# Hymba hybrid layer on one core: key and score slots padded from 4,224 to 4,352 bytes

## The chip, the cores and the metric

The kernel runs on one core of one Trainium2 chip. The metric is the device time of one execution in microseconds; lower is better. The time before is 1485.66 us, the median of 3 runs (1484.82 to 1486.38).

## The reference, cut to what matters

One decoder layer on 256 tokens of width 2,048, in float32. An input projection feeds two head groups side by side (a state-space part and a sparse attention), their outputs go through one output projection, and a convolutional feed-forward part with 5,632 channels follows.

```python
h = rms_norm(x, mix_norm_w)
proj = h @ w_in                                   # 2048 -> 10320 columns
z, xbc, dt_raw, q, kc, vc, ksl, vsl, kwn, vwn, gl = split(proj)
y_ssm  = rms_norm(ssd(silu(conv(xbc)), dt) * silu(z), ssm_norm_w)
y_attn = rms_norm(nsa_attention(q, kc, vc, ksl, vsl, kwn, vwn, gl), attn_norm_w)
x = x + concat([y_attn, y_ssm]) @ w_out           # 4096 -> 2048
u = conv(rms_norm(x, ffn_norm_w) @ w_up)          # 2048 -> 11264
gate, val = split(u, 2)
x = x + (silu(gate) * val) @ w_down               # 5632 -> 2048
return rms_norm(x, final_norm_w)
```

## The kernel before, in words

**The matmuls.** Every weight is read once from memory, in pieces of 512 KB (tile `raw`, 128 partitions x 1,024 floats). ScalarE rounds a piece to TensorE's reduced float32 (`whi`, fp32r), and VectorE forms what the rounding left (`wlo`). The activations are kept in the same two parts. A product is then three: high by high, high by low, low by high. A matmul here has a *stationary* operand, 128 columns that are loaded into the array (an LDWEIGHTS of its own), and a *moving* operand that streams past it, 512 or 256 columns. The 128 columns for the next matmul are loaded while the present one streams.

There are two layouts, and they swap the roles:

- **Channel pairs** (`chan_pair`, L332): the weights are stationary and the activations move. A step works on one piece. L343 issues 8 matmuls of 512 columns (4 slices of k by 2 blocks of channels; the moving tile is `hcat` or, in the feed-forward part, `hcatf`, high and low part side by side), and L346 issues 8 of 256 columns with `wlo` stationary. The 36 channel pairs of the input projection and the 44 of `w_up` have 4 steps each: 320 steps, 2,560 matmuls of 512 columns and 2,560 of 256. 56 of either kind, in the first steps, are recorded under L87, which is a helper's line.
- **Token groups**: the activations are stationary, 128 tokens at a time, and the weights move, always 512 columns. These are `tok_group` (L368, matmuls in L380 and L384) for the two value projections (stationary tile `hcat`) and for `w_out` (stationary `ya`, the attention's half, and `ys`, the state-space half), `prod_steps` (L1110, matmuls in L1122 and L1125) for `w_down` (stationary `act`), and `seven_steps` (L1159, matmuls in L1170 to L1172), which saves products in `w_down` by sums of activations (stationary `act` or `sums`). Together 1,965 matmuls of 512 columns. A step of `tok_group` or `prod_steps` has 8 matmuls with `whi` and then 4 with `wlo`.

**The order of the work.** One list of steps sets it. Step i's matmuls are issued in program order; its load is issued 7 steps ahead, its rounding 3 steps ahead (`LOADS`, `AHEAD`, L29). Side work (attention, state-space heads, convolutions) is cut into pieces that are issued between steps. The order of `w_down` is the string in L1353: p is a pair of steps of `prod_steps` on one `act` tile (act6, act7, act8, then act9 and so on), s is `seven_steps` on act0, act1 and so on, 21 matmuls each.

**The places in SBUF.** Most tiles live in the pool `gp` (L55) under fixed slots: `big(n, ...)` is slot Gn and `wide(n, ...)` is slot Hn. A slot is as large as its largest tile, and slots lie one behind the other in the order of their first use; the pools `stage` (tiles `raw`, `whi`, `wlo`) and `tmp` follow. All partitions have the same layout. Most slots have 4,096 or 8,192 bytes, whole multiples of 256. Two kinds of tile are 4,224 bytes, 16.5 times 256: `kcat` (keys, L633, slots G20 to G23) and `p1` (scores, L741, slots G27 and G28). Behind each of these six slots the addresses move by half of 256.

The addresses in the built program, from the start of a partition, with their remainder modulo 256:

| slots, in the order of their places | tiles that a large matmul reads there | before | after |
|---|---|---|---|
| G33, G16 | act21; xdt0, v00, ya0, act4 | 224 | 224 |
| G20 (4,224 bytes before) | kcat0, ya8, act8 | 224 | 224 |
| H0 to H3 | hcat, hcatf, sums2, sums3 | 96 | 224 |
| G12 to G15 | bc, blk | 96 | 224 |
| G17 to G19, G24 to G26 | v, ya2 to ya6, qp, ys0 to ys4, act5 to act7, act12 to act14 | 96 | 224 |
| G27 (4,224 before) | ys6, act15 | 96 | 224 |
| G28 (4,224 before) | ys8, act16 | 224 | 224 |
| G29, G30, G31, G8, G32, G9, G10, G11 | ys10 to ys14, pt, act0 to act3, act17 to act20 | 96 | 224 |
| G21 (4,224 before) | kcat1, ya10, act9 | 96 | 224 |
| G22 (4,224 before) | kcat2, ya12, act10 | 224 | 224 |
| G23 (4,224 before) | kcat3, ya14, act11 | 96 | 224 |
| pool stage | raw, whi, wlo | 224 | 224 |
| pool tmp | rt, u, acc, gate, bc1 (hold some of the sums) | 224 | 224 |

Inside these tiles the operands of the large matmuls start at multiples of 512 bytes, so an operand has its tile's remainder. In the table's terms, a large matmul's two operands lie **half a turn apart** (224 and 96) or at the **same remainder** (224 and 224).

Before, all 5,120 matmuls of the channel pairs are half a turn apart (`whi` or `wlo` at 224, `hcat` at 96). Of the 1,965 of the token groups 1,518 are half a turn apart, and 447 are at the same remainder: those with ya0, ya8, ya12, ys8, act4, act8, act10, act16, act21 and the sums in the pool tmp as the stationary tile.

Of the kernel before, what the change touches and what calls it, by code (L numbers as in the profile page):

```python
# [10 lines left out]
F32 = mybir.dt.float32  # L11
F32R = mybir.dt.float32r
# [4 lines left out]
P = 128  # L17
# [25 lines left out]
def hymba_kernel(  # L43
# [18 lines left out]
    def big(slot, shape, dtype, name):  # L62
        return gp.tile(shape, dtype, tag=f"G{slot}", name=name)
# [28 lines left out]
    def split(hi, lo, src):  # L92
        A.activation(hi, src, AF.Copy)
        V.tensor_tensor(lo, src, hi.bitcast(F32), op=ALU.subtract)
# [378 lines left out]
    def join_x(ps, scale=None, out_=None):  # L473

        u = join(ps, scale, out_)
        V.tensor_tensor(u, u, r1bc[0], op=ALU.mult)
        return u
# [115 lines left out]
    kcat = [None] * NG  # L593
# [35 lines left out]
    def kx_evac(b, g0):  # L629
        def evac(c, ps):  # L630
            g = g0 + c
            if kcat[g] is None:
                kt = big(20 + g, [P, 2, 528], F32R, f"kcat{g}")  # L633
                V.memset(kt[:, :, 15:16].bitcast(F32), 0.0)
                kcat[g] = kt
            u = join_x(ps).rearrange("p (s k) -> p s k", s=2)
            dv_ = [kcat[g][:, hl, 16:528].rearrange("p (s b k) -> p s b k", s=2, b=2)[:, :, b] for hl in range(2)]
            split(dv_[0], dv_[1], u)
        return evac
# [98 lines left out]
    def attention(g):  # L738
        q = [qp[2 * g], qp[2 * g + 1]]
        p0 = big(29, [P, 4, 272], F32, "p0")  # L740
        p1 = [big(27 + i, [P, 2, 528], F32, f"p1{i}") for i in range(2)]  # L741
        nm = [tmp.tile([P, 4, 3], F32, tag=f"nm{t}", name=f"nm{t}", bufs=1) for t in range(NT)]
        sm = [tmp.tile([P, 4, 3], F32, tag=f"sm{t}", name=f"sm{t}", bufs=1) for t in range(NT)]
        slope = [2.0 ** (-0.5 * (4 * g + h + 1)) for h in range(4)]
# [155 lines left out]
    def q_evac(pr):  # L900
        def evac(c, ps):
            if c == 0:
                if pr >= 3:
                    while (pr - 3) // 2 not in scored:
                        tick(1)
                qp[pr] = big(24 + pr % 3, [P, 2, 2, L], F32R, "qp")
            u = join_x(ps, scale=SCALE)
            split(qp[pr][:, c, 0], qp[pr][:, c, 1], u)
            if pr % 2 == 1 and c == 1:
                aux.append(attention(pr // 2))  # L910
        return evac
# [607 lines left out]
```

## Time and profile before

| | |
|---|---|
| median of 3 runs | 1485.66 us |
| the profiled execution, from its first to its last instruction | 1483.0 us |
| what lies around that span, against the median | 2.7 us |
| TensorE busy, matmuls | 1470.2 us of the span (99%) |
| VectorE busy | 1152.9 us (78%) |
| ScalarE busy | 889.0 us (60%) |
| DMA engines, share | about 60%, 188 GB/s |

How to read it: the duration that the profile gives for a matmul is from its start to its modelled end, some 390 ns for 512 columns, and neighbours overlap, so it is not what a matmul costs. What one costs in a dense stream is the distance from its start to the start of the next. The timeline merges equal matmuls into one row (start, length, count), so that the distance between the starts of two rows, divided by the matmuls in between, is the cost of one. Buffer numbers are left out in the profile: `act` is any of act0 to act21, and which one it is follows from the order of the steps.

### The profile page before, as it was taken

What the parts mean: (1) busy time and instruction counts of PE and PEld (TensorE: products, weight loads), DVE (VectorE), ACT (ScalarE), POOL (GpSimd) and SP (SyncE); (2) the same over time, 40 slices, a digit from 0 to 9 for tenths busy, and PEclk for the clock granted to TensorE, in tenths of its full rate; (3) what the DMA queues carried; (4) which work ended last, traced back from release to release, by engine and by line L of the source; (5) the groups of instructions that cost most, each with busy time, mean ns of one, the idle gap of its engine ahead of it and who ended that gap; (6) DMA issues with size and microseconds to landing.
All of it is one profiled execution on the core that took longest, in us unless ns stands there. A gap on an engine that the chain in (4) does not pass through costs nothing.

```text
span 1483.0 us, 21817 instructions
## 1 busy us (share of the span) xinstructions
PE 1470.2 (99%) x7936; PEld 1254.5 (85%) x7936; DVE 1152.9 (78%) x1894; ACT 889.0 (60%) x1446; POOL 3.6 (0%) x19
## 2 busy tenths in 40 slices
PE   9999999999999999999999999999999999999997
PEld 8888888888888888888888888888888888788886
DVE  7999799866898898555477777777777779978777
ACT  6768556655677697444365555555555556555544
POOL 0000000000000000000000000000000000000000
PEclk9999999999999999999999999999999999999999
DMA  8666667775454546555556666666656665565664
GB/s 256 170 189 209 199 192 237 228 230 157 143 143 135 168 138 216 186 186 188 190 173 191 190 184 186 187 186 195 186 185 186 189 194 185 192 210 188 204 199 142
DMA packets 222683, 278.47 MB, mean 188 GB/s; under 512 B 13176, under 2 KB 186864, under 8 KB 222448
## 3 DMA queue, kind: packets, MB, share of 16 engines
q1 hardware_dynamic: 220800, 272.59, 59.3%
q10 hardware_dynamic: 1776, 4.50, 0.9%
q8 instruction: 62, 1.02, 0.3%
q14 instruction: 45, 0.37, 0.1%
HBM read 274.92 MB, written 2.13 MB: 187 GB/s over the span
## 4 chain that ended last, share of the span: by engine, by line
PE 93%; DVE 3%; DMA 1%; ACT 1%; issue 1%; DVEq 0%; ACTq 0%; SPq 0%
PE mm L343 37%; PE mm L346 19%; PE mm L380 10%; PE mm L384 5%; PE aux L1122 4%; PE mm L1122 3%; PE aux L1125 2%; PE mm L1125 2%; DVE wlo L320 1%; DMA raw<-in_w_in_dram 1%; PE aux L1172 1%; PE aux L1171 1%; PE mm L1172 1%; PE aux L1170 1%; PE mm L1170 1%
## 5 line engine op out<-in xcount | busy, mean ns | idle before, releaser
L320 DVE TENSOR_TENSOR wlo<-raw,whi 128x1024 fp32r<-128x1024 f32 x408 | 496.9, 1221 | 244.6 <-ACT whi L314 243.1
L314 ACT ACTIVATE whi<-raw 128x1024 fp32r<-128x1024 f32 x408 | 430.7, 1057 | 412.9 <-PE mm L343 218.7
L343 PE MATMUL mm<-hcatf,whi 128*128 128x512 f32 x1408 | 356.8, 395 | 0.0
L343 PEld LDWEIGHTS mm<-hcatf,whi 128*128 128x128 f32 x1408 | 252.7, 188 | 46.5
L343 PE MATMUL mm<-hcat,whi 128*128 128x512 f32 x1096 | 282.4, 397 | 0.0
L343 PEld LDWEIGHTS mm<-hcat,whi 128*128 128x128 f32 x1096 | 197.7, 188 | 37.4 <-ACT rt L361 0.3
L346 PEld LDWEIGHTS mm<-hcatf,wlo 128*128 128x128 f32 x1408 | 191.7, 188 | 16.2
L346 PE MATMUL mm<-hcatf,wlo 128*128 128x256 f32 x1408 | 195.8, 282 | 0.0
L346 PEld LDWEIGHTS mm<-hcat,wlo 128*128 128x128 f32 x1096 | 149.6, 188 | 12.3
L346 PE MATMUL mm<-hcat,wlo 128*128 128x256 f32 x1096 | 153.8, 282 | 0.0
L1148 ACT ACTIVATE whi<-raw 128x1024 fp32r<-128x1024 f32 x88 | 91.6, 1057 | 67.4 <-DVE raw L1203 18.8
L1154 DVE TENSOR_TENSOR wlo<-raw,whi 128x1024 fp32r<-128x1024 f32 x88 | 105.4, 1221 | 12.6 <-ACT whi L1148 11.8
L380 PE MATMUL mm<-whi,ya 128*128 128x512 f32 x256 | 66.4, 398 | 0.0
L380 PE MATMUL mm<-whi,ys 128*128 128x512 f32 x256 | 64.5, 394 | 0.0
L1122 PE MATMUL aux<-whi,act 128*128 128x512 f32 x256 | 64.4, 394 | 0.0
L1122 PE MATMUL mm<-whi,act 128*128 128x512 f32 x232 | 59.5, 394 | 0.0
L380 PEld LDWEIGHTS mm<-whi,ys 128*128 128x128 f32 x256 | 48.2, 188 | 11.1
L1122 PEld LDWEIGHTS aux<-whi,act 128*128 128x128 f32 x256 | 48.1, 188 | 10.9
L380 PEld LDWEIGHTS mm<-whi,ya 128*128 128x128 f32 x256 | 47.3, 189 | 10.1
L1122 PEld LDWEIGHTS mm<-whi,act 128*128 128x128 f32 x232 | 43.7, 188 | 9.9
L362 DVE TENSOR_TENSOR u<-mm,rt 128x256 f32<-128x256 f32 x136 | 51.1, 417 | 0.2
L361 ACT ACTIVATE rt<-mm 128x256 f32<-128x256 f32 x144 | 46.6, 371 | 3.4 <-PE mm L346 2.2
(398 smaller groups left out, 1778.7 us busy)
## 6 DMA issues: line engine op xcount, KB each, us to landing
raw<-in_w_up_dram SPq DMA_DIRECT2D x176, 512.0 KB, 3.6
raw<-in_w_in_dram SPq DMA_DIRECT2D x160, 512.0 KB, 4.0
raw<-in_w_down_dram SPq DMA_DIRECT2D x88, 512.0 KB, 5.1
raw<-in_w_out_dram SPq DMA_DIRECT2D x64, 512.0 KB, 3.7
acq<-acum_d ACTq DMA_DIRECT2D x8, 512.0 KB, 5.8
raw<-in_cmp_w_k_dram SPq DMA_DIRECT2D x8, 512.0 KB, 4.6
raw<-in_cmp_w_v_dram SPq DMA_DIRECT2D x8, 512.0 KB, 4.6
x<-in_x_dram SPq DMA_DIRECT2D x4, 512.0 KB, 7.0
```

Source lines behind the costliest of these rows:

```text
L314: A.activation(hv, s.raw, AF.Copy)
L320: V.tensor_tensor(lv, s.raw, s.w[0].bitcast(F32), op=ALU.subtract)
L343: T.matmul(st["ps"][c], hv[:, kl, c * P:(c + 1) * P], k_of(k), start=(k == 0), stop=False)
L346: T.matmul(st["ps"][c][:, 256:512], lv[:, kl, c * P:(c + 1) * P], k_of(k)[:, 0, :], start=False, stop=(k == nk - 1))
L361: A.activation(rt, ps[:, 256:512], AF.Copy)
L362: V.tensor_tensor(u, ps[:, 0:256], rt, op=ALU.add)
L380: T.matmul(st["ps"][t], act(k)[:, hl, t * P:(t + 1) * P], hv[:, kl], start=(k == 0 and hl == 0), stop=False)
L384: T.matmul(st["ps"][t], act(k)[:, 0, t * P:(t + 1) * P], lv[:, kl], start=False, stop=(k == nk - 1))
L1122: T.matmul(x_[2 * t + n], act(k)[:, hl, t * P:(t + 1) * P], hv[:, n], start=(first and kl == 0 and hl == 0), stop=False)
L1125: T.matmul(x_[2 * t + n], act(k)[:, 0, t * P:(t + 1) * P], lv[:, n], start=False, stop=(last and kl == 1))
L1148: A.activation(hv[:, 0:n], src()[:, 0:n], AF.Copy)
L1154: V.tensor_tensor(lv[:, 0:n], src()[:, 0:n], s.w[0].bitcast(F32)[:, 0:n], op=ALU.subtract)
```

## The change

Two shapes grow from 528 to 544 floats in the last dimension. The 16 added floats are never read or written: all views end at column 528 as before. The six slots G20 to G23, G27 and G28 grow from 4,224 to 4,352 bytes (17 times 256), slot G29 keeps its 4,352, and everything behind the first of them moves up by 128 to 768 bytes. The instructions, their order on every engine, their shapes and their waits are the same in both programs; only addresses differ.

```diff
@@ -630,7 +630,7 @@
         def evac(c, ps):
             g = g0 + c
             if kcat[g] is None:
-                kt = big(20 + g, [P, 2, 528], F32R, f"kcat{g}")
+                kt = big(20 + g, [P, 2, 544], F32R, f"kcat{g}")
                 V.memset(kt[:, :, 15:16].bitcast(F32), 0.0)
                 kcat[g] = kt
@@ -738,7 +738,7 @@
     def attention(g):
         q = [qp[2 * g], qp[2 * g + 1]]
         p0 = big(29, [P, 4, 272], F32, "p0")
-        p1 = [big(27 + i, [P, 2, 528], F32, f"p1{i}") for i in range(2)]
+        p1 = [big(27 + i, [P, 2, 544], F32, f"p1{i}") for i in range(2)]
```

## The prediction

> **What bounds the kernel now.** First the profile's page: the span, the engines, the granted clock, the costliest groups.
>
> ```profile
> span 1483.0 us, 21817 instructions
> PE 1470.2 (99%) x7936; PEld 1254.5 (85%) x7936; DVE 1152.9 (78%) x1894; ACT 889.0 (60%) x1446; POOL 3.6 (0%) x19
> PEclk9999999999999999999999999999999999999999
> ...
> L343 PE MATMUL mm<-hcatf,whi 128*128 128x512 f32 x1408 | 356.8, 395 | 0.0
> ...
> L346 PE MATMUL mm<-hcatf,wlo 128*128 128x256 f32 x1408 | 195.8, 282 | 0.0
> ```
>
> TensorE is busy from end to end at the full clock (9 is 90% or more). The last number of a group is its idle time: 0.0 us in front of both. The chain that ended last runs 93% through TensorE, and of all groups of TensorE waits the longest comes to 1.4 us:
>
> ```profile
> PE 93%; DVE 3%; DMA 1%; ACT 1%; issue 1%; DVEq 0%; ACTq 0%; SPq 0%
> ```
>
> ```profile
> PE aux L497 <- DVE bc L94: 1.4, 1, 1.4
> ```
>
> So the time is the sum of what the matmuls cost, start to start. What one costs is in the timeline of TensorE (start in us, length, count). First a stretch of w_down, where the weights stream and the activations are stationary. By the order of L1353 it begins inside act7's pair of steps; then come act8's two steps, 21 matmuls on act0, act9's two steps and act10's first.
>
> ```profile
> 1247.27 2.02 PE L1122 MATMUL aux<-whi,act 128*128 128x512 f32 x8
> 1249.13 1.08 PE L1125 MATMUL aux<-wlo,act 128*128 128x512 f32 x4
> 1250.05 1.98 PE L1122 MATMUL aux<-whi,act 128*128 128x512 f32 x8
> 1251.86 1.07 PE L1125 MATMUL aux<-wlo,act 128*128 128x512 f32 x4
> 1252.77 1.98 PE L1122 MATMUL aux<-whi,act 128*128 128x512 f32 x8
> ...
> 1255.49 0.41 PE L1170 MATMUL mm<-whi,act 128*128 128x512 f32 x1
> ...
> 1260.37 2.03 PE L1122 MATMUL aux<-whi,act 128*128 128x512 f32 x8
> ...
> 1265.96 1.99 PE L1122 MATMUL aux<-whi,act 128*128 128x512 f32 x8
> 1267.79 1.07 PE L1125 MATMUL aux<-wlo,act 128*128 128x512 f32 x4
> 1268.69 1.52 PE L1122 MATMUL aux<-whi,act 128*128 128x512 f32 x6
> ```
>
> A step has 12 equal matmuls. act7's last step takes 1250.05 - 1247.27 = 2.78 us, or 231.7 ns for each. Both of act8's take 2.72 us (1252.77 - 1250.05, 1255.49 - 1252.77): 226.7 ns. act9's take 5.59 us for two (1265.96 - 1260.37), 2.795 each: 232.9 ns. act10's first takes 2.73 us. Same instructions, same engines at work beside them, clock the same. What differs is the table of addresses: act8 and act10 lie at 224 modulo 256, as the moving whi and wlo do, while act7 and act9 lie at 96. With both operands at one remainder a matmul of 512 columns costs 226.7 ns; half a turn apart it costs about 232.5. That is what the change can earn, since it brings every large pair to one remainder.
>
> The gain needs a run-in. In w_out, ys8 and ya8 are both at 224 as well; here are, by the order of the steps, a step of ys8 and then the first step of ya8 on its second visit:
>
> ```profile
> 595.33 1.98 PE L380 MATMUL mm<-whi,ys 128*128 128x512 f32 x8
> 597.15 1.08 PE L384 MATMUL mm<-wlo,ys 128*128 128x512 f32 x4
> ```
>
> ```profile
> 618.50 2.01 PE L380 MATMUL mm<-whi,ya 128*128 128x512 f32 x8
> 620.36 1.08 PE L384 MATMUL mm<-wlo,ya 128*128 128x512 f32 x4
> 621.27 1.10 PE L380 MATMUL mm<-whi,ya 128*128 128x512 f32 x4
> ```
>
> ys8's first 8 take 1.82 us, 227.5 ns each. ya8's first 8 take 1.86 us, 232.5 ns each, as if half a turn apart; its last 4 take 0.91, 227.5 each. So the equal remainder does nothing at once: the stream slides into a state without loss, after one matmul or only after eight, as the matmuls before have left it, and then it stays.
>
> **The change, part by part.** No instruction is added, taken away or moved; the order on all five engines is the same in both programs, and the 16 added floats are touched by nobody. What moves is addresses. Three terms.
>
> *Token groups.* Of their 1,965 matmuls 1,518 are half a turn apart now. Each is to go from 232.5 to 226.7 ns: 1,518 x 5.8 = 8.8 us. These are long rows of 512-column matmuls alone, so the good state is seldom left; I take off 0.8 us for steps that follow other work. The 447 pairs that are equal already gain where they now run in (like ya8): 0.6 us. Together **8.6 us**. Bounds: 7 (a tenth to a quarter lost to run-in) to 9.4.
>
> *Channel pairs, 512 columns.* Here both operands always lie half a turn apart, so no row shows the pair at one remainder. Two steps of w_up:
>
> ```profile
> 884.85 2.03 PE L343 MATMUL mm<-hcatf,whi 128*128 128x512 f32 x8
> 886.71 1.12 PE L346 MATMUL mm<-hcatf,wlo 128*128 128x256 f32 x8
> 887.67 2.02 PE L343 MATMUL mm<-hcatf,whi 128*128 128x512 f32 x8
> 889.52 1.10 PE L346 MATMUL mm<-hcatf,wlo 128*128 128x256 f32 x8
> 890.47 2.03 PE L343 MATMUL mm<-hcatf,whi 128*128 128x512 f32 x8
> ```
>
> The eight take 1.86 and 1.85 us, 231.9 ns each in the mean. The bounds are 226.7 (settled from the first) and 232.5 (ya8: run-in takes all eight). The four rows above in which a first eight at one remainder follows something else are act8 with 1.81 us (1251.86 - 1250.05), act10 with 1.83, ys8 with 1.82 and ya8 with 1.86; their mean is 1.83, or 228.8 ns. I take -3.1 ns, to which 0.5 is added because the eight here come after matmuls that were already at one remainder: -3.6 ns x 2,560 = **9.2 us** (bounds 0 to 13.3).
>
> *Channel pairs, 256 columns.* The eight of L346 take 0.96 and 0.95 us above, 119.4 ns each, more than half of what 512 columns cost. If they settle too, 226.7 / 2 = 113.3 ns is the floor, my estimate from act8's rows: -6.1. The nearest rows at one remainder are the last matmuls, 256 columns each, three on a piece, first two pieces with act20 (half a turn apart), then two with act21 (equal):
>
> ```profile
> 1472.01 0.41 PE L1392 MATMUL mm<-whi,act 128*128 128x256 f32 x2
> ...
> 1472.74 0.40 PE L1392 MATMUL mm<-whi,act 128*128 128x256 f32 x2
> ...
> 1473.45 0.41 PE L1392 MATMUL aux<-whi,act 128*128 128x256 f32 x2
> ...
> 1474.16 0.40 PE L1392 MATMUL aux<-whi,act 128*128 128x256 f32 x2
> ```
>
> Six take 0.73 us half a turn apart, then 0.71 equal, then 0.71 half a turn apart: 121.7, 118.3, 118.3 ns. So six matmuls gain between nothing and 3.4 ns, far from the floor. I take -1.7, the middle of that: 2,560 x 1.7 = **4.4 us** (bounds -15.6 to +5.9, the latter by 121.7 ns).
>
> *What is late next.* A faster TensorE leaves the others less time. The tightest stretch is that of the state-space heads:
>
> ```profile
> 222.00:259.00 37.00, 37.00 (x238) 31.84 (x238) 36.32 (x68) 24.37 (x32) 0.00 (x0) 1.00 0.77 236
> ```
>
> VectorE is busy for 36.32 of 37 us there, 0.7 us of room, and TensorE would want about 0.6 (37 x 21/1483). Some pieces will be late, and their users wait: **0.8 us** given back. In the rest of the program VectorE is at 78% in the mean, and rounding runs three steps ahead.
>
> The sum: 8.6 + 9.2 + 4.4 - 0.8 = 21.4 us. The profiled span goes from 1483.0 to 1461.6 us; with the 2.7 us by which the median of the runs is above that span, 1464.3 us, rounded to **1464**.
>
> A rule of the Trainium skill speaks against all of this. Its page "TensorE: Matmul & The Clock Gate", in the section "Step-by-step: what each phase is for", gives TensorE two independent read ports into SBUF, one for the streaming operand and one for the weights, and says that loading the next tile's weights takes nothing from the running matmul. By it the sum would be 0 and the time 1485.7; the rows of act7 to act10 disagree by 5.8 ns a matmul.
>
> **The rivals.**
>
> *Both kinds settle for good.* If the good state survives the 256-column matmuls as it survives the change from L1122 to L1125, a step of a channel pair costs 8 x 226.7 + 8 x 113.3 = 2,720 ns instead of the 2,810 above (890.47 - 884.85 is 5.62 us for two): 320 x 0.09 = 28.8 us, with the token groups 37.4, less 1.5 for a VectorE that now binds in the tight stretch. That is 1449.8 us. For it: act8 keeps the state through 24 matmuls and over a change of moving tile. Against: the last rows, where 256 columns show little.
>
> *Only the token groups gain.* The 256-column matmuls throw the stream out of step each time, and the next eight spend themselves on the run-in, like ya8. 1485.7 - 8.6 = 1477.1 us. For it: ya8 itself. Against: three of four runs-in were shorter.
>
> *The remainder is not the cause.* Then act8, act10 and ys8 are quick for another reason, and the time stays at 1485.7. Against: all three are at 224, and act7 and act9, which are not, show nothing. By the rule of the Trainium skill cited above ("TensorE: Matmul & The Clock Gate") this would be the case.
>
> *Slower.* Today VectorE writes wlo and ScalarE whi at 224 while TensorE streams hcat at 96. After the change all three walk the same remainders in the channel pairs, 320 steps long. If each matmul there loses as much to those writes as an unequal pair loses now, 5.8 ns, it is 5,120 x 5.8 = 29.7 us, less 8.6: 1506.8 us. It decides from 8.6 / 5,120 = 1.7 ns a matmul. Against: in act8's steps the writers work at 224 next to two TensorE operands at 224, and these are the quickest rows of all.
>
> **How the numbers follow.** What this measurement can tell from no change is about 0.2%, 3 us. My forecast, 1464 with 1456 to 1473 of its own: 0.48. Both settle, 1450: 0.30. Token groups alone, 1477: 0.13. No effect: 0.04. Slower, 1507: 0.05. The range reaches from just under the second case to just over the third, 1448 to 1478, and leaves out about 0.1. Faster by over 0.2% are the first three, 0.91; the same 0.04; slower 0.05.
>
> **What would show each step right or wrong.** In the timeline after, a `prod_steps` step should be 2.72 us for every act tile, act9 as act8; if act9's still takes 2.79, the remainder is not the cause. A step of w_up should take about 2.81 - 8 x 0.0036 - 8 x 0.0017 = 2.77 us. 2.72 would be the second case, 2.81 the third, 2.83 and more the fourth. The first eight of L343 against the eight of L346 show which of the two terms is mis-sized. VectorE's waits and a TensorE wait in the stretch from 222 us on would show the room running out. The prediction is wrong if the steps of w_up do not move, or if TensorE waits eat what they gain.

## The result, and the profile after

The changed kernel takes 1474.19 us (median of 4 runs, 1472.43 to 1474.76); the kernel before took 1485.78 us beside it. The ratio is 0.9917 (95% interval 0.9905 to 0.993). That is 11.6 us faster: inside the range of 1448 to 1478, 10 us short of the forecast of 1464, and a little above the 1456 to 1473 that the forecast allowed itself. The profiled execution took 1474.53 us, its span 1472.8 us, 10.2 us less than before.

The first lines of the page of after, with the two large groups and the start of the chain:

```profile
span 1472.8 us, 21817 instructions
PE 1458.7 (99%) x7936; PEld 1255.7 (85%) x7936; DVE 1152.1 (78%) x1894; ACT 889.0 (60%) x1446; POOL 3.6 (0%) x19
PEclk9999999999999999999999999999999999999999
...
PE 93%; DVE 4%; DMA 1%; issue 1%; ACT 1%; DVEq 0%; ACTq 0%; SPq 0%
...
L343 PE MATMUL mm<-hcatf,whi 128*128 128x512 f32 x1408 | 353.0, 392 | 0.0
...
L346 PE MATMUL mm<-hcatf,wlo 128*128 128x256 f32 x1408 | 196.6, 282 | 0.0
```

The instructions are as many, TensorE is busy as before, and the page shows the full clock. L343's group fell by 3.8 us of busy time; L346's *rose* by 0.8.

The first check that the prediction named is `prod_steps`. The same stretch of w_down in the timeline of TensorE after, from act7's last step through act8, the seven-matmul steps on act0, act9 and act10's first:

```profile
1239.63 1.98 PE L1122 MATMUL aux<-whi,act 128*128 128x512 f32 x8
...
1242.35 1.98 PE L1122 MATMUL aux<-whi,act 128*128 128x512 f32 x8
...
1245.07 1.98 PE L1122 MATMUL aux<-whi,act 128*128 128x512 f32 x8
...
1247.79 0.39 PE L1170 MATMUL mm<-whi,act 128*128 128x512 f32 x1
...
1252.55 1.98 PE L1122 MATMUL aux<-whi,act 128*128 128x512 f32 x8
...
1255.27 1.98 PE L1122 MATMUL aux<-whi,act 128*128 128x512 f32 x8
...
1257.99 1.98 PE L1122 MATMUL aux<-whi,act 128*128 128x512 f32 x8
...
1260.71 1.07 PE L1122 MATMUL aux<-whi,act 128*128 128x512 f32 x4
```

Every step takes 2.72 us (1242.35 - 1239.63, and so on), act9's like act8's, and the 21 matmuls between them 4.76 us: 226.7 ns each. This part came as forecast.

The second check is w_up:

```profile
879.49 2.00 PE L343 MATMUL mm<-hcatf,whi 128*128 128x512 f32 x8
881.33 1.12 PE L346 MATMUL mm<-hcatf,wlo 128*128 128x256 f32 x8
882.28 2.00 PE L343 MATMUL mm<-hcatf,whi 128*128 128x512 f32 x8
884.12 1.11 PE L346 MATMUL mm<-hcatf,wlo 128*128 128x256 f32 x8
885.07 2.00 PE L343 MATMUL mm<-hcatf,whi 128*128 128x512 f32 x8
```

A step takes 2.79 us (885.07 - 879.49 = 5.58 for two), where 2.77 was forecast and 2.81 stood before. The eight of 512 columns take 1.84 us, 230.1 ns each. The eight of 256 take 0.95, 119 each. From start to start, the matmuls of one settled step are, in ns:

| | 1st | 2nd | 3rd | 4th | 5th | 6th | 7th | 8th |
|---|---|---|---|---|---|---|---|---|
| 512 columns (L343) | 233.3 | 235.8 | 228.3 | 232.5 | 230.8 | 226.7 | 226.7 | 226.7 |
| 256 columns (L346) | 113.3 | 119.2 | 120.0 | 120.0 | 120.0 | 120.0 | 120.0 | 120.0 |

Five matmuls of run-in, three settled ones, one short one of 256, and then the 256s settle at 120.0; the eight average 119.1, where they averaged 118.5 before. All but one of the 174 undisturbed steps of w_up take 2,793 or 2,794 ns.

The third check is the waits of TensorE after, the longest and the four in w_down (us in total, times, longest):

```profile
PE aux L497 <- DVE bc L94: 1.6, 1, 1.6
...
PE aux L1125 <- DVE wlo L1154: 0.5, 1, 0.5
PE aux L1172 <- DVE wlo L1154: 0.4, 1, 0.4
...
PE mm L1172 <- DVE wlo L1154: 0.3, 1, 0.3
...
PE mm L1125 <- DVE wlo L1154: 0.2, 1, 0.2
```

The four on `wlo` (0.5 + 0.4 + 0.3 + 0.2 = 1.4 us) are new. They lie in w_down, where the faster TensorE catches up with VectorE's rounding, and not in the stretch from 222 us on, where the prediction looked for them.

By stage, from the first large matmul of one stage to that of the next, the input projection from the span's start (us):

| | input projection | w_out | w_up | w_down to the end | span |
|---|---|---|---|---|---|
| before | 560.95 | 181.69 | 496.27 | 244.13 | 1483.0 |
| after | 559.89 | 178.17 | 493.39 | 241.36 | 1472.8 |
| difference | -1.06 | -3.52 | -2.88 | -2.77 | -10.2 |

### The profile page after: what moved, and what is told of

The parts are those of the page before. It is cut to its first block, busy times and chain, and to the rows that moved or that the text cites. A ratio compares the mean times of both kernels' runs of the same rounds, so it can differ in the third digit from the quotient of the medians.

```text
span 1472.8 us, 21817 instructions
## 1 busy us (share of the span) xinstructions
PE 1458.7 (99%) x7936; PEld 1255.7 (85%) x7936; DVE 1152.1 (78%) x1894; ACT 889.0 (60%) x1446; POOL 3.6 (0%) x19
## 4 chain that ended last, share of the span: by engine, by line
PE 93%; DVE 4%; DMA 1%; issue 1%; ACT 1%; DVEq 0%; ACTq 0%; SPq 0%
PE mm L343 37%; PE mm L346 19%; PE mm L380 10%; PE mm L384 5%; PE aux L1122 3%; PE mm L1122 3%; PE mm L1125 2%; PE aux L1125 2%; PE mm L87 1%; DVE wlo L320 1%; PE aux L815 1%; DVE wlo L1154 1%; PE aux L1170 1%; PE aux L1172 1%; PE aux L1171 1%
## 5 line engine op out<-in xcount | busy, mean ns | idle before, releaser
L343 PE MATMUL mm<-hcatf,whi 128*128 128x512 f32 x1408 | 353.0, 392 | 0.0
L343 PEld LDWEIGHTS mm<-hcatf,whi 128*128 128x128 f32 x1408 | 253.2, 189 | 45.2
L343 PE MATMUL mm<-hcat,whi 128*128 128x512 f32 x1096 | 279.9, 394 | 0.0
L343 PEld LDWEIGHTS mm<-hcat,whi 128*128 128x128 f32 x1096 | 197.5, 188 | 36.6 <-issue 0.3
L346 PEld LDWEIGHTS mm<-hcatf,wlo 128*128 128x128 f32 x1408 | 192.2, 190 | 13.7
L346 PE MATMUL mm<-hcatf,wlo 128*128 128x256 f32 x1408 | 196.6, 282 | 0.0
L346 PEld LDWEIGHTS mm<-hcat,wlo 128*128 128x128 f32 x1096 | 149.9, 190 | 11.0
L346 PE MATMUL mm<-hcat,wlo 128*128 128x256 f32 x1096 | 154.0, 282 | 0.0
L1154 DVE TENSOR_TENSOR wlo<-raw,whi 128x1024 fp32r<-128x1024 f32 x88 | 105.3, 1221 | 11.4 <-ACT whi L1148 10.3
```

Of the source, the lines that this page charges most:

```text
L343: T.matmul(st["ps"][c], hv[:, kl, c * P:(c + 1) * P], k_of(k), start=(k == 0), stop=False)
L346: T.matmul(st["ps"][c][:, 256:512], lv[:, kl, c * P:(c + 1) * P], k_of(k)[:, 0, :], start=False, stop=(k == nk - 1))
L1154: V.tensor_tensor(lv[:, 0:n], src()[:, 0:n], s.w[0].bitcast(F32)[:, 0:n], op=ALU.subtract)
```

## The experiments

Theory A is the prediction's: what a large matmul costs hangs on how the places of its two operands lie to each other modulo 256, within TensorE alone. Theory B is that the writers (ScalarE, VectorE) or the loads at the same remainders set it. *Lag* below is the remainder of the stationary operand less that of the moving one, modulo 256.

### TensorE by itself

This kernel leaves out the whole layer. TensorE runs alone over operands that nobody writes any more, in blocks of 32 matmuls; the PSUM tile's name tells the lag, from `none` (0) over `one` (32 bytes) and `half` (128) to `seven` (224).

```python
shifted = lambda e: (lambda i: 8 * e + 128 * (i % 8))
for n in (512, 256):
    for e in range(8):
        block(e, n, 32, s=shifted(e))
for e in (0, 4):
    for r in range(8):
        for n in (512, 256):
            block(e, n, 8, s=shifted(e))
...
block(7, 512, 32)
```

> Leaves out the whole layer: only matmuls from two prepared tiles, in blocks of 32, no other engine at work beside them. Theory A (the two operands of TensorE, their remainders modulo 256 bytes against each other, set the cost; alone, without any other engine): blocks of 512 columns cost 226.7 ns a matmul at the same remainder after a run-in of at most 9 matmuls, and 231 to 234 ns half a turn apart; 256 columns cost 120.0 ns at the same remainder and 118 to 119.5 half a turn apart; eight of 512 and eight of 256 in turn at the same remainder cost 1.84 and 0.95 us as in w_up after the change. Theory B (writers: VectorE and ScalarE writes into tiles at the same or another remainder make the difference): no difference between the blocks here, 226.7 ns or less for 512 columns and 113.3 for 256 in all of them.

Its timeline. The first block of `none` is not used: its first matmuls take 427 ns each, which is the start of the clock. The last row, named `seven`, is its repetition at lag 0. The rows of 128 hold eight turns of eight matmuls of 512 and eight of 256, a step of a channel pair:

```profile
51.94 7.59 PE L67 MATMUL half<-mov,sta 128*128 128x512 f32 x32
...
66.83 7.49 PE L67 MATMUL six<-mov,sta 128*128 128x512 f32 x32
...
81.63 3.99 PE L67 MATMUL none<-mov,sta 128*128 128x256 f32 x32
85.46 3.95 PE L67 MATMUL one<-mov,sta 128*128 128x256 f32 x32
...
111.99 22.51 PE L67 MATMUL none<-mov,sta 128*128 128x512 f32 x128
134.34 22.65 PE L67 MATMUL half<-mov,sta 128*128 128x512 f32 x128
156.84 39.55 PE L67 MATMUL none<-mov,sta 128*128 128x128 f32 x288
...
281.10 7.44 PE L67 MATMUL seven<-mov,sta 128*128 128x512 f32 x32
```

With 512 columns a block takes 7.44 us at lag 0 and 7.59 at half a turn; the settled matmuls within them take 226.7 and 232.1 ns. Other lags give 233 to 234, and `six` (192 bytes) 228.7. With 256 columns lag 0 gives 3.83 us (85.46 - 81.63), 120.0 ns settled: about the same as `half`'s 120.1, for which 118 to 119.5 had been expected, and more than the 117.3 to 118.3 of five other lags. Eight and eight in turn take 2.794 us at lag 0 (134.34 - 111.99 = 22.35 for eight turns) and 2.81 at half a turn (22.50): the steps of w_up after and before, to the nanosecond. At half a turn the turns alternate between 2,799 and 2,821 ns, and so do the steps of w_up before. A holds and B falls: no writer and no transfer is there. And the smaller gain of the channel pairs needs nothing but TensorE.

### The other way to one remainder

The kernel before with one padded key slot (the last), so that the stages `raw`, `whi`, `wlo` and the pool tmp move down to the 96 where most activations lie, and not these up to 224. Since the sums in tmp move too, 402 matmuls of the token groups come to lie half a turn apart, and not the 447 of the expectation.

```diff
-                kt = big(20 + g, [P, 2, 528], F32R, f"kcat{g}")
+                kt = big(20 + g, [P, 2, 544 if g == 3 else 528], F32R, f"kcat{g}")
```

> The kernel before with raw, whi and wlo moved by half a turn, to 96; hcat stays at 96, the token groups' stationary tiles stay where they were (most at 96, five slots at 224). Theory A (equal remainder counts, not which one): the channel pairs as after the change, 2.79 us a step of w_up; a prod_steps step of w_down takes 2.72 us on act7 and act9 and 2.79 us on act8 and act10, the reverse of before; 447 matmuls of the token groups are now half a turn apart at 5.8 ns, 2.6 us, so 1476 to 1478 us. Theory C (224 itself is a good place, whatever the other operand's): slower or the same as before, 1485 us or more, act8 still quicker than act7.

1476.18 us, ratio 0.9937 (0.9923 to 0.9951); w_up takes 493.39 us, as after. Now act8 and act10, quick before, must be slow. The timeline from act8's first step on:

```profile
1242.81 2.03 PE L1122 MATMUL aux<-whi,act 128*128 128x512 f32 x8
...
1245.61 2.02 PE L1122 MATMUL aux<-whi,act 128*128 128x512 f32 x8
...
1248.40 0.39 PE L1170 MATMUL mm<-whi,act 128*128 128x512 f32 x1
...
1253.17 1.98 PE L1122 MATMUL aux<-whi,act 128*128 128x512 f32 x8
...
1255.89 1.98 PE L1122 MATMUL aux<-whi,act 128*128 128x512 f32 x8
...
1258.62 2.03 PE L1122 MATMUL aux<-whi,act 128*128 128x512 f32 x8
...
1261.41 2.02 PE L1122 MATMUL aux<-whi,act 128*128 128x512 f32 x8
```

act8's two steps take 2.80 and 2.79 us, act9's 2.72 and 2.73, act10's first 2.79: the pattern of before turned round. It is not 224 that is good, it is the same remainder.

### hcat alone

The kernel before with only the four `hcat` slots moved to 224. The activations of w_out and w_down keep the places of before, except sums2 and sums3, which lie in the same slots.

```diff
-    hc = [wide(i, [P, 4, 2, L], F32R, f"hcat{i}") for i in range(4)]
+    hc = [wide(i, [P, 2080 if i == 3 else 2048], F32R, f"hcat{i}")[:, 0:2048].rearrange("p (k h t) -> p k h t", k=4, h=2)
+          for i in range(4)]
...
-                kt = big(20 + g, [P, 2, 528], F32R, f"kcat{g}")
+                kt = big(20 + g, [P, 2, 544 if g == 0 else 528], F32R, f"kcat{g}")
```

> The kernel before with the four hcat slots alone moved to 224; every other tile keeps its remainder (most stationary tiles of the token groups stay at 96, half a turn from whi). Theory A (each pair of operands for itself): the channel pairs as after the change, 2.79 us a step of w_up, 320 x 0.017 = 5.4 us; the 192 matmuls of the two value projections gain 1.1 us; w_out and w_down as before. About 1479 us. If the channel pairs gain nothing by themselves (Rival E: all of the gain is the token groups') it stays at 1486.

1481.17 us, ratio 0.9968 (0.9956 to 0.998): 4.6 us of the 11.6 come with `hcat`. About 1479 had been expected; in the profiled execution the first 33 us took 1.3 us more than before, which is explained further down, and w_down 0.5 us more. Its w_up takes 493.39 us as after, its w_out 181.63 as before. Its steps of w_up are after's, 2.79 us:

```profile
877.49 2.00 PE L344 MATMUL mm<-hcatf,whi 128*128 128x512 f32 x8
...
880.28 2.00 PE L344 MATMUL mm<-hcatf,whi 128*128 128x512 f32 x8
```

### 512 columns in place of 256

Do the 256s break the good state, or does the change from `whi` to `wlo`? After, with L346 over all 512 columns (low by low is multiplied too, which is extra work).

```diff
-                        T.matmul(st["ps"][c][:, 256:512], lv[:, kl, c * P:(c + 1) * P], k_of(k)[:, 0, :],
+                        T.matmul(st["ps"][c], lv[:, kl, c * P:(c + 1) * P], k_of(k),
```

> The changed kernel, with the low-weight matmuls of the channel pairs over all 512 columns instead of 256 (it adds the low-by-low product, more work). Theory A (the matmuls of 256 columns push the stream out of its settled state, and each next eight pay the run-in): all 16 matmuls of a step cost 226.7 ns, a step of w_up 3.63 us, no run-in at the first eight; with 320 steps x (3.63 - 2.79) about 1741 us. Rival D (the change of the stationary tile from wlo to whi, or of the part of the PSUM bank, costs the run-in): the first eight still cost 1.84 us, a step 3.65 us or more.

1739.76 us. One step of its w_up, and the start of the next:

```profile
900.96 1.98 PE L343 MATMUL mm<-hcatf,whi 128*128 128x512 f32 x8
902.77 1.98 PE L346 MATMUL mm<-hcatf,wlo 128*128 128x512 f32 x8
904.59 1.98 PE L343 MATMUL mm<-hcatf,whi 128*128 128x512 f32 x8
```

A step is 3.63 us (3,627 ns in the mean), 226.7 ns for each of its 16: no run-in at all. So the width breaks the state, not the change of weights, and L343 would have earned its full gain beside neighbours of 512 columns. Which half of the PSUM bank the 256s write does not matter: in the layer it is the second, with TensorE alone the first, and both cost the same step.

### A map of the lags, twice

Is there a pair of lags, one for the 512s and one for the 256s, that suits both? These two kernels again leave out the layer: TensorE alone, steps of eight and eight in turn, three (then four) for each pair. The first takes every 32 bytes, and ahead of that has rows of 40 matmuls of one width at finer lags; the second takes 15 lags of the 512s and nine of the 256s, near the best.

```python
for e in range(0, 64, 8):
    for f in range(0, 64, 8):
        for r in range(3):
            block(f // 8, 512, 8, s=lambda i: e + 128 * i)
            block(f // 8, 256, 8, m=lambda i: 512 * (i % 4), s=lambda i: f + 1024 + 256 * (i % 4) + 128 * (i // 4))
```

> Leaves out the whole layer: matmuls from two prepared tiles, the stationary operand at a lag behind the moving one of 0 to 240 bytes in steps of 16 (and at 4, 8, 12, 120, 136, 188 and 196), blocks of 40 with 512 and with 256 columns; then eight of 512 and eight of 256 in turn, with every pair of lags in steps of 32. Theory A: the cost is a function of the lag modulo 256 alone; 512 columns 226.7 at lag 0, 228.7 at 192 with no run-in, 232 to 234 at the other multiples of 32; 256 columns 120.0 at 0 and 117.3 to 118.3 at 32 to 96, 192 and 224. In turn: 8 x 228.7 + 8 x 117.6 = 2.77 us with the weights at a lag of 192 in the first eight, against 2.79 at 0 and 2.81 at 128, so there should be a place for hcat that is better than the change's. If the run-in is a matter of the number of columns alone, no pair of lags does better than 2.79.

Rows of the first map, three steps each: (0, 0), (128, 128) and (192, 64) bytes, the 512s' lag first, each with the row behind it, whose start ends it. A row's name tells the 256s' lag:

```profile
344.87 8.55 PE L67 MATMUL none<-mov,sta 128*128 128x512 f32 x48
353.26 8.54 PE L67 MATMUL one<-mov,sta 128*128 128x512 f32 x48
...
647.68 8.59 PE L67 MATMUL half<-mov,sta 128*128 128x512 f32 x48
656.11 8.61 PE L67 MATMUL five<-mov,sta 128*128 128x512 f32 x48
...
765.53 8.40 PE L67 MATMUL two<-mov,sta 128*128 128x512 f32 x48
773.77 8.49 PE L67 MATMUL three<-mov,sta 128*128 128x512 f32 x48
```

8.39, 8.43 and 8.24 us: 2.80, 2.81 and 2.75 a step. Over all 64 pairs the middle step of the three lies between 2.747 and 2.833 us; (0, 0), the change's pair, is the twelfth at 2.791, and (192, 64) is the best. With the 512s at 192 and the 256s at 32, 64, 96, 192 or 224 the settled prices of the single widths had let 2.77 be expected; these five take 2.747 to 2.806. What a pair costs in turn is not the sum of what its two lags cost in long rows.

> Leaves out the whole layer: eight matmuls of 512 columns and eight of 256 in turn, four times over for each of 15 lags of the first and 9 of the second, around the good places of the coarse map (0, 120, 192; 8, 64, 208 to 224). Theory A: the good places are narrow and a matter of 4 to 16 bytes; the best pair comes to 2.72 us (226.7 and 113.3 ns, nothing lost), more likely 2.74. If the map were smooth, neighbours of 192 and 64 would lie within 0.01 us of 2.747.

In the second map (192, 64) stays best at 2.746 us. 4 or 8 bytes beside it a step costs 2.760 to 2.806, so the good places are narrow; none came to the 2.720 of the prediction's second case.

### The best pair in the kernel

After, with `hcat` at 32 (sums2 and sums3, in the same slots, too) and, in the channel pairs alone, `wlo` at 96: lag 192 for L343's line and 64 for L346's (here L344 and L347).

```diff
+    hc = [wide(i, [P, 2096 if i == 3 else 2048], F32R, f"hcat{i}")[:, 0:2048].rearrange("p (k h t) -> p k h t", k=4, h=2)
...
-                lo = stage.tile([P, 1024], F32R, tag="lo", name="wlo", bufs=SPLITS)
-                lv = lo[:, :kh * ncol].rearrange("p (k c) -> p k c", k=kh)
+                lo = stage.tile([P, 1088], F32R, tag="lo", name="wlo", bufs=SPLITS)
+                lv = lo[:, shift:shift + kh * ncol].rearrange("p (k c) -> p k c", k=kh)
...
-                kt = big(20 + g, [P, 2, 544], F32R, f"kcat{g}")
+                kt = big(20 + g, [P, 2, 552 if g == 0 else 544], F32R, f"kcat{g}")
```

> The changed kernel with hcat at 32 instead of 224 and, in the channel pairs alone, wlo at 96, so that the weights lie 192 bytes (high) and 64 bytes (low) behind hcat; the token groups keep 224 for both operands. One tile of 1 KB is moved into another's place to make room. Theory A (the lag modulo 256 sets the cost, in the layer as in the strip of matmuls): a step of w_up takes 2.75 us instead of 2.79, as this pair of lags did in the strip, the first eight about 1.835 us, the eight low ones about 0.912; 320 x 0.045 = 14 us less than the change, less 1 us for the value projections, whose hcat is now 64 from whi: about 1461 us. Rival F (the equal remainder is what pays and any unequal one costs): 2.81 us a step or more, 1480 us. Rival G (VectorE has no room left): the steps shorten but TensorE waits; 1465 us or more.

1465.41 us, ratio 0.9865 (0.9848 to 0.9881): faster than both kernels. Its w_up in the timeline, and the longest waits of its TensorE:

```profile
870.84 2.00 PE L344 MATMUL mm<-hcatf,whi 128*128 128x512 f32 x8
872.68 1.07 PE L347 MATMUL mm<-hcatf,wlo 128*128 128x256 f32 x8
873.59 2.00 PE L344 MATMUL mm<-hcatf,whi 128*128 128x512 f32 x8
```

```profile
PE aux L528 <- ACT xs L582: 2.3, 2, 1.9
PE aux L498 <- DVE bc L94: 1.9, 1, 1.9
PE aux L87 <- DVE r_r L87: 1.7, 1, 1.7
```

A step is 2.75 us, as TensorE alone had given; w_up takes 485.27 us, 8.1 less than after. But about 1461 us had been expected. The input projection gave nothing: 561.69 us, 1.8 more than after, and its first 33 us are 0.1 of that. Behind them, held against after from start to start of the same matmul, the 256s save 3.1 us, and more than this is lost again in four places:

- 1.7 us of longer waits. TensorE's waits ahead of w_down come to 8.7 us, 4.7 after, so that the case of a VectorE without room is borne out in part.
- 1.5 us at half clock, in 13 matmuls from 59.73 us on, right behind the wait of 1.95 us on `bc`:

```profile
59.80:63.22 3.42, 3.42 (x12) 0.50 0.91 229
```

- 1.0 us in the value projections, whose operands now lie at a lag of 64.
- 0.5 us in the 512s. Of the 118 steps whose 16 matmuls stand together, 47 take up to 2,764 ns, 49 take 2,765 to 2,835 and 22 more than that. After other work the stream needs a step or two to come back to 2.75 (from 331.55 us on the steps take 2.82, 2.77, 2.75), and between attention's matmuls it mostly does not get there.

In the row above, 0.50 is the granted clock. Behind the wait of 1.90 us at 117 us it stays at 1.00, and so it does in after, behind 1.57 us on `bc`. This is one execution, the slowest of the four (1467.52 us); whether the others had the half clock too is not known.

## Why the prediction was right, and where its size was off

All differences below are sums over the trace, from start to start of the same matmul before and after, in us (the terms are rounded, so their sum is 0.1 off the span's 10.2):

| term | forecast | measured |
|---|---|---|
| token groups, without new waits | -8.6 | -8.5 (w_out 3.5, w_down 4.2, value projections 0.8) |
| channel pairs, 512 columns | -9.2 | -6.0 |
| channel pairs, 256 columns | -4.4 | +1.5 |
| waits given back | +0.8 | +1.4 |
| the first 33 us | 0 | +1.3 |
| sum | -21.4 | -10.3 |

That the time stayed within the range is owed to the range's width, which took in the case of the token groups alone: the gain is about half of the forecast one, and of its terms only one came at its price.

**The cause: right.** The rows of act7 to act10 were read rightly; the reversed pattern with the stages at 96 and TensorE alone both show it. So the rival in which the remainder is not the cause is out. The Trainium skill's two independent read ports, one for each operand ("TensorE: Matmul & The Clock Gate", "Step-by-step: what each phase is for"), don't describe this: by them the lag would change nothing, and with only TensorE at work it changes a matmul of 512 columns from 226.7 to 232 ns and more.

**Token groups: right in size.** 8.5 us of 8.6.

**Channel pairs, 512 columns: mis-sized.** The step that failed is the 228.8 ns taken from four first eights, and the 0.5 ns taken off besides. Those eights came after matmuls of 512 columns. Here each eight comes after eight of 256, pays five matmuls of run-in and averages 230.1 instead of the 228.3 forecast. The price before was mis-read as well: 231.9 from two steps, where the mean of w_up is 232.7. Together that is -2.6 ns in w_up instead of -3.6, and less in the input projection. The kernel with 512 columns everywhere shows what is missing: there nothing is paid. The third case ("the 256-column matmuls throw the stream out of step each time") had the mechanism, but not its size: five of the eight are lost, not all.

**Channel pairs, 256 columns: wrong sign.** The last rows of the program, six matmuls at a time, were too short to settle. In w_up the 256s went from 118.5 ns in the mean to 119.1, so the equal remainder costs 0.6 ns each; the 119.4 of the prediction came from two steps. The settled price does not tell this, since long rows cost 120.0 ns at lag 0 and 120.1 at half a turn: it is the turn of eight and eight that is dearer, 953 ns against 948 for the eight 256s with TensorE alone too. The term was within the bounds. That 512 and 256 columns have different best lags had not been thought of. Together with the 512s, a step of w_up went to 2.793 us instead of 2.77, and all 320 steps gained 4.5 us, where 13.6 had been forecast.

**What is late next: wrong place.** In the tight stretch VectorE is busy for 36.28 of 37 us after and TensorE does not wait there; the waits came in w_down, 1.4 us.

**The writers (slower): out.** After, all three walk the same remainders in 320 steps, and a step is quicker; TensorE alone gives the same 2.79 us without any writer.

**The first 33 us** took 1.3 us more, and what differs there is the start of the clock. Eight transposes at 5 us took 1.10 us in the profiled execution of before and 1.97 in that of after:

```profile
5.19 1.10 PE L87 MATMUL aux<-ident,x 128*128 128x128 f32 x8 [0.51 <-DMA x<-in_x_dram]
```

```profile
5.16 1.97 PE L87 MATMUL aux<-ident,x 128*128 128x128 f32 x8 [0.48 <-DMA x<-in_x_dram]
```

The views give a granted clock of 1.00 at 5 us in both, but that is no reading: they give 1.00 wherever the trace holds no record of the clock. The records begin, with the full clock, at 4.8 us in before, 4.2 with 512 columns and 5.2 with the best pair, ahead of these transposes, which take 1.1 us there; and at 10.4 in after, 9.7 with `hcat` alone and 9.2 with the stages at 96, behind them, and there they take 1.97. The kernel with 512 columns has the change's addresses and an early clock, so these addresses do not bring the late one. Each program was profiled once, so that one and the same program starts both ways is not shown. The Trainium skill has TensorE start at half its clock until it was busy for one window that runs on freely, so that the point varies from execution to execution ("TensorE: Matmul & The Clock Gate", "What's actually happening"). These rows agree with it in that: at one and the same place some executions show about 250 ns a transpose and others 137. But the Trainium skill has the point vary by about half a microsecond, and here it lies between 4.2 and 10.4 us. The late clock hides 1.3 us of what the change earns in the span.

## What to carry to other kernels

When TensorE is busy from end to end, place its two operands as deliberately as its buffers: look in the timeline for equal matmuls of unequal cost from start to start and hold them against the table of addresses. The best place has to be measured per width and per sequence, with TensorE alone and the layer's own pattern of widths; the number found that way held to the nanosecond in long rows of steps and did not hold where other matmuls come between. A price read from a handful of matmuls is no price of a settled row, and the price of a settled row of one width is no price of two widths in turn.

## What the runs showed of the hardware

- The cost of one of these matmuls (fp32r, with a weight load of its own) depends on the lag of its operands modulo 256 and on what ran before. At 512 columns, settled: 226.7 ns at lag 0, 16 and 120 bytes, 228.7 at 192, 228.3 to 230.7 at 8, 12, 176 and 240, 232 to 234 at the others. At 256 columns: 120.0 at lag 0 and 128, 113.3 to 123.3 elsewhere; lag 64 stood at 117.8 in the first kernel of TensorE alone and at 113.3 in the first map, so one lag can hold more than one state.
- 113.3, 120.0, 226.7 and 233.3 ns are 17, 18, 34 and 35 times 6.67 ns. That was noticed, not explained; what inside TensorE's reading makes the lag count stays open.
- With a weight load for each matmul, 128, 192, 224 and 240 columns all cost 111.6 to 112.0 ns (TensorE alone, lags 0 and 128): from 240 columns down to 128, fewer columns save nothing.
- The granted clock fell to 0.50 for 3.4 us behind a wait of TensorE of 1.95 us, and not behind one of 1.90 us in the same execution (best pair).
